# Block products of w_out and w_ffn_out in a decoder layer: eight multiplications of half-size blocks become seven

## The chip, the cores and the metric

One core of a Trainium2 chip runs the whole layer in one launch. The metric is the device time of one execution in microseconds (us); the kernel before took 893.11 us (median of three runs, 893.06 to 895.8).

## The reference, cut to what matters

One layer of a decoder works on 512 tokens with 1024 channels, all in float32. Only two of its many matrix products change, `merged @ w_out` and the second product of the SwiGLU:

```python
x = x + merged @ w_out[i]                          # 512x1024 @ 1024x1024
hf = rms_norm(x, norm_ffn[i]) @ w_ffn_in[i]
x = x + (jax.nn.silu(hf[..., :FFN_HIDDEN]) * hf[..., FFN_HIDDEN:]) @ w_ffn_out[i]   # 512x2816 @ 2816x1024
pg = jax.nn.sigmoid(rms_norm(x, norm_ple[i]) @ w_ple_gate[i])
x = x + pg * (p[i] @ w_ple_proj[i])
```

Ahead of them stand the input projection with its three branches (an SSM, a short convolution, sliding-window attention) and their gates; behind them the embedding gate (`w_ple_gate`) and a final norm.

## The kernel before, in words

Every float32 operand is split into two float32r parts, a high part `hi` (a copy by ACT, L206 for weights and L244 for activations) and the remainder `lo` (a subtraction by DVE, L207 and L245). A product is the sum of three matmuls, high by high, low by high and high by low (L248 to L250 where the result is channels by tokens, L1214 to L1216 where it is tokens by channels). So each 128x128 by 128x512 piece costs three matmuls.

Weights come as a stream of slabs of 1 MB (`add_slab`, L121). SP issues their loads (`emit_load`, L179, the DMA on L184) into two `raw` buffers. A slab is cut into two halves of 128x1024; `emit_split` (L187) writes the copy and, four steps later, the subtraction, into one of the pairs of `hi` and `lo` buffers: four pairs (`hla`) at first, seven from w_out on (`hlb`). `group` takes the next halves, `retire` and `ahead` write the split of a later half as soon as a pair of buffers is done with. So up to three halves (six later) are ready ahead of TensorE.

The order of work is written out by hand: each engine takes its instructions in program order, and a semaphore wait holds up everything behind it on that engine. `pump` counts three-matmul steps, and `later(d, fn)` puts an instruction of another engine d steps further on. A buffer that is used again makes its new writer wait until all readers of the old content are done.

The stages around the change are these. `branch` (L1145) makes `merged`, [1024 channels, 512 tokens], two 128-channel blocks at a time, each from 24 matmuls behind a gate product of 48, and splits them into `mh` and `ml`. `td_gemm` (L1230) multiplies them by w_out: four token tiles of 128 by two column halves of 512. Column half 0 runs with the weights outside (`td_outer_k`, four PSUM banks at once), column half 1 token tile by token tile; `accum` (L1209, the DVE addition on L1211) adds each finished bank into `xr`, the residual, which is loaded anew at L1205. After each tile of column half 1 `Norm.pre` (L1253) queues the norm of that tile: Square on ACT (L1261), mean on DVE (L1264), power on POOL (L1265), scaling on DVE (L1272) and eight transposes on PE (L325), at the steps 1, 3, 4, 9 and 10 of `NORM_AT`. The normed activations go into `h` and `l` (`hpool`, one buffer each, which hold the normed input of the whole first phase before).

The SwiGLU runs in three chunks of 8, 8 and 6 hidden 128-blocks (`CHUNKS`): a chunk makes its activations `gh`, `gl` from w_ffn_in (L1288 on) and multiplies them at once by its rows of w_ffn_out with `td_gemm`. The last chunk's column half 1 carries the norm for the embedding gate. That last stage needs `ppt` (2 MB) and a gain, both loaded in chunk 1.

Of the kernel before, what the change touches and what calls it, by code (L numbers as in the profile page):

```python
# [17 lines left out]
T = 512  # L18
D = 1024
# [56 lines left out]
def hybrid_trunk_kernel(  # L76
# [41 lines left out]
    halves = []  # L118
    slabs = []

    def add_slab(ap, k, n, axis):  # L121
        s = len(slabs)
        slabs.append(dict(ap=ap, k=k, n=n, raw=None))
        cnt = 2 if k * n == 2048 else 1
        for i in range(cnt):
            halves.append(dict(s=s, i=i, cnt=cnt, axis=axis, hl=None))
# [31 lines left out]
    for n in range(2):  # L158
        for kk in range(2):
            add_slab(kn(w_out[0][kk * 512:kk * 512 + 512, n * 512:n * 512 + 512]), 4, 512, "k")  # L160
    CHUNKS = [(0, 8), (8, 8), (16, 6)]
    for h0, hn in CHUNKS:
        for j in range(h0, h0 + hn, 2):
            for ab in range(2):
                c0 = ab * FFN + j * 128
                add_slab(kn(w_ffn_in[0][:, c0:c0 + 256]), 8, 256, "n")
        for n in range(2):
            for k0 in range(0, hn, 4):
                kq = min(4, hn - k0)
                r0 = (h0 + k0) * 128  # L170
                add_slab(kn(w_ffn_out[0][r0:r0 + kq * 128, n * 512:n * 512 + 512]), kq, 512, "k")
# [5 lines left out]
    state = dict(pump=0, delay=False, split=0, load=0, next=0, top=3, slot=0, pools=[hla] * 4)  # L177

    def emit_load():  # L179
        s = slabs[state["load"]]  # L180
        state["load"] += 1
        t = rawp.tile([128, 2048], F32, tag="raw", name="raw")
        v = t[:, 0:s["k"] * s["n"]].rearrange("p (k n) -> p k n", k=s["k"])
        sp.dma_start(out=v, in_=s["ap"])  # L184
        s["raw"] = v

    def emit_split():  # L187
        h = halves[state["split"]]
        state["split"] += 1
        while state["load"] <= h["s"]:  # L190
            emit_load()
        s = slabs[h["s"]]
        k, n, i = s["k"], s["n"], h["i"]
        if h["cnt"] == 1:
            src = s["raw"]
        elif h["axis"] == "n":
            n //= 2
            src = s["raw"][:, :, i * n:(i + 1) * n]
        else:
            k //= 2  # L200
            src = s["raw"][:, i * k:(i + 1) * k, :]
        pl = state["pools"][state["slot"] % len(state["pools"])]
        state["slot"] += 1
        hi = pl.tile([128, 1024], F32R, tag="hi", name="hi").rearrange("p (k n) -> p k n", k=k)
        lo = pl.tile([128, 1024], F32R, tag="lo", name="lo").rearrange("p (k n) -> p k n", k=k)
        act.copy(out=hi, in_=src)  # L206
        todo = [lambda: dve.tensor_tensor(lo, src, hi.bitcast(F32), ALU.subtract)]  # L207
        h["hl"], h["low"] = (hi, lo), lambda: todo and todo.pop()()
        later(LAG, h["low"])
# [177 lines left out]
    def prep_gen(tp):  # L387
        # per-channel vectors: ssm_d (4 tiles) and the conv taps (3 x 4 tiles)
# [59 lines left out]
    def prep_fine(tp, lt, ldt, T1, T2, tabs):  # L448
# [73 lines left out]
        # coefficients  # L522
# [85 lines left out]
    # the tensor engine's clock rises only under load  # L608
# [347 lines left out]
    # chunks of 4 tokens; channels of a group pair and the time in the chunk share the partitions  # L956
    def ssm_gen(ct):
# [69 lines left out]
        # the two row halves of the array write to banks of their own  # L1027
# [117 lines left out]
    def branch(d0, sgs, yh, yl, mode, mh=None, ml=None):  # L1145
        hl = take()
        for i in range(2):
# [8 lines left out]
            if mode == 2:  # L1156
                split_ap(merged[:, d], mh[:, d], ml[:, d])
# [42 lines left out]
    xp = open_pool(ctx, "xres")  # L1200
    hlb = open_pool(ctx, "hlb", 3)
    state["pools"] = [hla] * 4 + [hlb] * 3
    state["slot"] = 4
# [14 lines left out]
    def td_outer_k(ah, al, kn_, n):  # L1218
        pss = [ps_z() for _ in range(4)]
        for h in range(kn_ // 2):  # L1220
            hi, lo = take()
            for t in range(4):
                for k in range(2):
                    kk = 2 * h + k
                    td_mm(pss[t], ah, al, kk, slice(t * 128, (t + 1) * 128), hi, lo, k, kk == kn_ - 1)
                    pump()
        for t in range(4):
            accum(t, n, pss[t])

    def td_gemm(ah, al, kn_, pre_fn=None):  # L1230
        td_outer_k(ah, al, kn_, 0)
        if pre_fn is None:
            td_outer_k(ah, al, kn_, 1)
            return
        nh = kn_ // 2
        h0 = group(nh)
        for t in range(4):
# [184 lines left out]
```

## Time and profile before

| | us |
|---|---|
| median of 3 runs | 893.11 |
| span of the profiled execution, first to last instruction | 892.6 |
| TensorE busy in that span | 874.4 |
| VectorE, ScalarE, GpSimd busy | 491.1, 341.0, 95.9 |

The page gives the span of the profiled execution and no other time of it; the median lies 0.5 us above that span. PE is TensorE's matmuls, PEld its weight loads, DVE VectorE, ACT ScalarE, POOL GpSimd, SP the engine that issues the loads. Matmuls overlap in the pipeline, so the duration of one (0.39 us) is longer than the distance between the starts of two. A row of a timeline gives the start, the duration, the engine and the line; in square brackets stands how long the engine had been idle and who ended that.

### The profile page before, as it was taken

Reading aid. Unit: us, or ns where it says so; the run is one execution under the profiler, and the core shown is the slowest. Engines: PE = TensorE matmul, PEld = TensorE weight load, DVE = VectorE, ACT = ScalarE, POOL = GpSimd, SP = SyncE. Lnnn points to the kernel's source line nnn. Section 1 sums busy time; section 2 is a strip of 40 time slices with the busy share of each in tenths; the row PEclk is TensorE's granted clock in tenths of the full one; section 3 lists DMA queues with packets and bytes.
Section 4 is the critical chain, followed back from the end, with each engine's and each line's share of the span. In section 5 each row is a group of like instructions: output and inputs, shape, how many; then the busy total and the mean of one; then the engine's idle time right before and its main releaser. Section 6 shows DMA issues by size and latency. Waiting matters only on the chain.

```text
span 892.6 us, 10527 instructions
## 1 busy us (share of the span) xinstructions
PE 874.4 (98%) x4143; PEld 715.2 (80%) x4143; DVE 491.1 (55%) x737; ACT 341.0 (38%) x546; POOL 95.9 (11%) x86
## 2 busy tenths in 40 slices
PE   8999999999999979999999999999999999999997
PEld 6988787877777758888889888888888888888886
DVE  3789698948588585554545433333333333334654
ACT  5665556445443343433334322212222212222533
POOL 1030061713123030000000000000000000000000
PEclk9999999999999989999999999999999999999998
DMA  8756511253634523223813322222225332233002
GB/s 300 216 189 218 195 59 30 66 173 113 178 95 156 156 94 107 95 79 134 284 46 107 130 94 95 95 95 94 95 95 211 99 100 87 72 120 110 29 1 94
DMA packets 84849, 107.25 MB, mean 120 GB/s; under 512 B 6120, under 2 KB 66176, under 8 KB 84288
## 3 DMA queue, kind: packets, MB, share of 16 engines
q1 hardware_dynamic: 84800, 106.59, 36.5%
q8 instruction: 32, 0.52, 0.2%
q14 instruction: 17, 0.14, 0.1%
HBM read 94.83 MB, written 11.55 MB: 119 GB/s over the span
## 4 chain that ended last, share of the span: by engine, by line
PE 77%; DVE 10%; issue 4%; ACT 3%; DMA 3%; SPq 1%; POOL 1%; POOLq 0%; DVEq 0%; ACTq 0%
PE z L248 17%; PE z L249 16%; PE z L250 16%; PE z L1216 8%; PE z L1215 8%; PE z L1214 8%; DVE lo L207 1%; DVE s_t L839 1%; DMA xt<-in_x_dram 1%; PE t L325 1%; DVE s_t L812 1%; DMA raw<-in_w_in_dram 1%; POOL gsw L1063 1%; ACT s_t L826 1%; PE t L1084 1%
## 5 line engine op out<-in xcount | busy, mean ns | idle before, releaser
L248 PE MATMUL z<-h,hi 128*128 128x512 f32 (+1 forms) x776 | 298.6, 385 | 0.0
L207 DVE TENSOR_TENSOR lo<-raw,hi 128x1024 fp32r<-128x1024 f32 x142 | 177.6, 1253 | 216.2 <-ACT hi L206 216.1
L249 PE MATMUL z<-l,hi 128*128 128x512 f32 (+1 forms) x776 | 292.2, 377 | 0.0
L250 PE MATMUL z<-h,lo 128*128 128x512 f32 (+1 forms) x776 | 292.1, 376 | 0.0
L206 ACT CAST hi<-raw 128x1024 fp32r<-128x1024 f32 x142 | 148.2, 1047 | 133.1 <-PE z L1216 87.2
L248 PEld LDWEIGHTS z<-h,hi 128*128 128x128 f32 x776 | 146.8, 189 | 29.9 <-issue 3.7
L250 PEld LDWEIGHTS z<-h,lo 128*128 128x128 f32 x776 | 146.7, 189 | 27.6
L249 PEld LDWEIGHTS z<-l,hi 128*128 128x128 f32 x776 | 147.0, 189 | 24.7
L1214 PE MATMUL z<-hi,gh 128*128 128x512 f32 x176 | 69.5, 395 | 0.0
L1216 PE MATMUL z<-hi,gl 128*128 128x512 f32 x176 | 69.1, 393 | 0.0
L1215 PE MATMUL z<-lo,gh 128*128 128x512 f32 x176 | 69.1, 392 | 0.0
L1265 POOL TENSOR_TENSOR rs<-ms,nhalf 128x1 f32<-128x1 f32 x8 | 4.4, 550 | 487.2 <-DVE ms L1264 487.2
L244 ACT CAST gh<-sil 128x512 fp32r<-128x512 f32 x22 | 13.6, 620 | 86.0 <-DVE sil L1319 86.0
L248 PE MATMUL z<-yh,hi 128*128 128x512 f32 x112 | 45.1, 403 | 0.0
L249 PE MATMUL z<-yl,hi 128*128 128x512 f32 x112 | 44.2, 395 | 0.1
L250 PE MATMUL z<-yh,lo 128*128 128x512 f32 x112 | 44.2, 395 | 0.0
L1310 ACT ACTIVATE sil<-z 128x512 f32<-128x512 f32 x22 | 13.2, 598 | 75.4 <-PE z L250 75.4
L1319 DVE TENSOR_TENSOR sil<-z,sil 128x512 f32<-128x512 f32 x22 | 15.2, 691 | 46.8 <-PE z L250 46.8
L1216 PEld LDWEIGHTS z<-hi,gl 128*128 128x128 f32 x176 | 33.1, 188 | 7.5
L1215 PEld LDWEIGHTS z<-lo,gh 128*128 128x128 f32 x176 | 33.1, 188 | 7.4
L1214 PEld LDWEIGHTS z<-hi,gh 128*128 128x128 f32 x176 | 33.1, 188 | 7.3
L1211 DVE TENSOR_TENSOR xr<-z,xr 128x512 f32<-128x512 f32 x32 | 21.5, 687 | 15.6 <-PE z L1216 15.5
(258 smaller groups left out, 1058.5 us busy)
## 6 DMA issues: line engine op xcount, KB each, us to landing
raw<-in_w_in_dram SPq DMA_DIRECT2D x23, 1024.0 KB, 5.5
raw<-in_w_ffn_in_dram SPq DMA_DIRECT2D x22, 1024.0 KB, 5.2
raw<-in_w_ffn_out_dram SPq DMA_DIRECT2D x10, 1024.0 KB, 5.0
raw<-in_w_branch_dram SPq DMA_DIRECT2D x12, 512.0 KB, 3.4
cs<-tb SPq DMA_DIRECT2D x4, 1024.0 KB, 5.2
raw<-in_w_out_dram SPq DMA_DIRECT2D x4, 1024.0 KB, 5.8
raw<-in_w_ple_gate_dram SPq DMA_DIRECT2D x4, 1024.0 KB, 5.1
xt<-in_x_dram SPq DMA_DIRECT2D x4, 512.0 KB, 9.4
```

Source lines behind the costliest of these rows:

```text
L206: act.copy(out=hi, in_=src)
L207: todo = [lambda: dve.tensor_tensor(lo, src, hi.bitcast(F32), ALU.subtract)]
L244: act.copy(out=hi, in_=src)
L248: pe.matmul(ps, wh, ah, start=first, stop=False)
L249: pe.matmul(ps, wh, al, start=False, stop=False)
L250: pe.matmul(ps, wl, ah, start=False, stop=last)
L1211: dve.tensor_tensor(dst, ps, dst, ALU.add)
L1214: pe.matmul(ps, ah[:, kk, ts], hi[:, k, ns], start=(kk == 0), stop=False)
L1215: pe.matmul(ps, ah[:, kk, ts], lo[:, k, ns], start=False, stop=False)
L1216: pe.matmul(ps, al[:, kk, ts], hi[:, k, ns], start=False, stop=last)
L1310: act.activation(out=s, in_=ps, func=AF.Silu)
L1319: dve.tensor_tensor(sil[i], ps, sil[i], ALU.mult)
```

## The change: what it does, and the diff

The four products (w_out, and the three chunks of w_ffn_out) are written as 2 by 2 blocks: two halves of 256 tokens, two halves of the inner dimension (alternating 128-blocks, `kt` of them each: 4, 4, 4 and 3) and two column halves of 512. Seven block products with sums of blocks take the place of eight. The sums of activation blocks are made by DVE in `forms`, which splits seven blocks (`fh`, `fl`) for each pair of 128-blocks in place of two. The sums of weight blocks are made by DMAs: `x` is B12, and B11 is added to it by a second DMA with `accum_op` ADD; when `x` has been split, B22 is added to it (`x+`), and when that has been split, B21. `y` is B12 plus B22. These DMAs are issued by POOL. A block product serves two token tiles, adds into PSUM banks that several products share, and after each product DVE adds the bank into `xr` or subtracts it. `x` and `y` of w_out lie in the buffers `h` and `l` of `hpool`; those of the chunks lie in a pool of their own and are issued four slabs early (`early=4`; 0 for w_out). The seven pairs of split buffers stay four until the embedding gate; `ppt` comes in four loads after chunk 2.

```diff
+    def add_block_product(w, r0, kt, early=4):
+        def blk(h, n):
+            v = w[r0:r0 + 2 * kt * 128, n * 512:n * 512 + 512].rearrange("(i h p) n -> h p i n", h=2, p=128)
+            return v[h]
+        at = len(loads) - early
+        kinds = (("raw", blk(0, 0)), ("raw", blk(1, 0)), ("x", (blk(0, 1), blk(0, 0))), ("raw", blk(1, 1)),
+                 ("x+", blk(1, 1)), ("y", (blk(0, 1), blk(1, 1))), ("x+", blk(1, 0)))
+        for kind, ap in kinds:
+            add_slab(ap, kt, 512, "k", kind, at if kind in ("x", "y") else None)
+
+    add_block_product(w_out[0], 0, 4, 0)
...
+        add_block_product(w_ffn_out[0], h0 * 128, hn // 2)
...
     def emit_load():
...
+            pl, tag = state["xy"][s["kind"]]
+            t = pl.tile([128, 2048], F32, tag=tag, name=s["kind"])
...
+            pool.dma_start(out=v, in_=s["ap"][0])
+            pool.dma_start(out=v, in_=s["ap"][1], accum_op=ALU.add)
...
+    def more_x(s):
+        for q in slabs[s + 1:s + 8]:
+            if q["kind"] == "x+" and q["raw"] is None:
+                pool.dma_start(out=state["x"], in_=q["ap"], accum_op=ALU.add)
...
+        def low():
+            dve.tensor_tensor(lo, src, hi.bitcast(F32), ALU.subtract)
+            if s["kind"] in ("x", "x+") and h["i"] == h["cnt"] - 1:
+                more_x(h["s"])
...
-            if mode == 2:
-                split_ap(merged[:, d], mh[:, d], ml[:, d])
+        if mode == 2:
+            forms(merged[:, d0:d0 + 2], d0 // 2)
...
+    def forms(g, i):
+        sums = fmp.tile([128, 4, 256], F32, tag="sums", name="sums")
+        g11, g12, g21, g22 = (g[:, h, o:o + 256] for o in (0, 256) for h in range(2))
+        split_ap(g[:, :, 0:256], fh[:, 0:2, i], fl[:, 0:2, i])
+        dve.tensor_tensor(sums[:, 0], g21, g22, ALU.subtract)
+        dve.tensor_tensor(sums[:, 1], sums[:, 0], g11, ALU.subtract)
+        dve.tensor_tensor(sums[:, 2], g11, g21, ALU.subtract)
+        dve.tensor_tensor(sums[:, 3], g12, sums[:, 1], ALU.add)
+        split_ap(sums, fh[:, 3:7, i], fl[:, 3:7, i])
+        split_ap(g22, fh[:, 2, i], fl[:, 2, i])
...
-    hlb = open_pool(ctx, "hlb", 3)
-    state["pools"] = [hla] * 4 + [hlb] * 3
...
+    PRODUCTS = ((A11, 0, True, 1, 0, 0), (A12, 2, True, 1, 0, 0), (FD, 1, True, 1, 1, 1), (S4, 1, False, 1, 0, 1),
+                (S2, 0, False, -1, 0, 1), (S3, 0, False, -1, 1, 1), (A22, 0, False, 1, 1, 0))
+
+    def block_product(kt, norm=None):
+        banks = {}
+        for i, (f, bk, first, sign, th, n) in enumerate(PRODUCTS):
+            if first:
+                banks[bk] = [(ps_t if bk == 2 else ps_z)() for _ in range(2)]
+            for q in range(2):
+                h0 = group(1)
+                if q == 0:
+                    ahead()
+                hi, lo = halves[h0]["hl"]
+                k0, kc = halves[h0]["part"][0:2]
+                for t in range(2):
+                    ps, ts = banks[bk][t], slice(t * 128, (t + 1) * 128)
+                    for k in range(kc):
...
+                        pe.matmul(ps, fh[:, f, kk, ts], hi[:, k], start=st, stop=False, skip_group_check=True)
+                        pe.matmul(ps, fl[:, f, kk, ts], hi[:, k], start=False, stop=False, skip_group_check=True)
+                        pe.matmul(ps, fh[:, f, kk, ts], lo[:, k], start=False, stop=last, skip_group_check=True)
+                        pump()
+                    if last:
+                        dst = xr[:, 2 * th + t, n * 512:(n + 1) * 512]
+                        dve.tensor_tensor(dst, ps if sign > 0 else dst, dst if sign > 0 else ps,
+                                          ALU.add if sign > 0 else ALU.subtract)
+                        if norm is not None and i in (4, 6):
+                            norm.pre(2 * th + t)
+                retire(h0)
...
-    td_gemm(mh, ml, 8, nf.pre)
+    block_product(4, nf)
...
-        if ci == 2:
-            td_gemm(gh, gl, hn, npl.pre)
-        else:
-            td_gemm(gh, gl, hn)
+            forms(g, j // 2)
+        block_product(hn // 2, npl if ci == 2 else None)
...
+    hlb = open_pool(ctx, "hlb", 3)
+    state["pools"] = [hla] * 4 + [hlb] * 3
...
+    for t in range(4):
+        sp.dma_start(out=ppt[:, t], in_=pp_d[t * 128:(t + 1) * 128, :])
```

## Rows read from the trace of the kernel before

**Rows 1.** The page: span, and busy time of the engines

```profile
span 892.6 us, 10527 instructions
...
PE 874.4 (98%) x4143; PEld 715.2 (80%) x4143; DVE 491.1 (55%) x737; ACT 341.0 (38%) x546; POOL 95.9 (11%) x86
```

**Rows 2.** Stretches: PE, PEld, DVE, ACT, POOL busy (count), PEclk, DMA share, GB/s

```profile
423.90:468.20 44.30, 44.30 (x201) 36.10 (x201) 22.00 (x28) 15.12 (x21) 1.66 (x3) 1.00 0.48 166
641.00:682.00 41.00, 41.00 (x180) 33.58 (x179) 14.11 (x15) 10.88 (x14) 0.00 (x0) 1.00 0.25 83
```

**Rows 3.** Groups by line and form: count, busy us, mean ns, then idle before

```profile
L207 DVE TENSOR_TENSOR lo<-raw,hi 128x1024 fp32r<-128x1024 f32 x142 | 177.6, 1253 | 216.2 <-ACT hi L206 216.1
L206 ACT CAST hi<-raw 128x1024 fp32r<-128x1024 f32 x142 | 148.2, 1047 | 133.1 <-PE z L1216 87.2 <-DMA raw<-in_w_in_dram 19.8 <-PE z L249 16.3
...
L1214 PE MATMUL z<-hi,gh 128*128 128x512 f32 x176 | 69.5, 395 | 0.0
...
L1214 PE MATMUL z<-hi,mh 128*128 128x512 f32 x64 | 25.5, 398 | 0.0
...
L1211 DVE TENSOR_TENSOR xr<-z,xr 128x512 f32<-128x512 f32 x32 | 21.5, 687 | 15.6 <-PE z L1216 15.5
...
L245 DVE TENSOR_TENSOR gl<-sil,gh 128x512 fp32r<-128x512 f32 x22 | 15.2, 693 | 15.3 <-ACT gh L244 15.3
```

**Rows 4.** Timeline of PE: last gate matmul, first of w_out, end of w_out's column half 0

```profile
418.13 0.39 PE L250 MATMUL z<-h,lo 128*128 128x512 f32 x1
...
423.95 0.39 PE L1214 MATMUL z<-hi,mh 128*128 128x512 f32 x1
...
446.00 0.39 PE L1216 MATMUL z<-hi,ml 128*128 128x512 f32 x1
```

**Rows 5.** Timeline of w_out's column half 1: a finished bank, its addition, the norm

```profile
451.54 0.39 PE L1216 MATMUL z<-hi,ml 128*128 128x512 f32 x1
...
451.97 0.69 DVE L1211 TENSOR_TENSOR xr<-z,xr 128x512 f32<-128x512 f32 x1 [3.23 <-PE z L1216]
...
452.70 1.06 ACT L1261 ACTIVATE xn<-xr 128x1024 f32<-128x1024 f32 x1 [5.21 <-DVE xr L1211]
...
454.11 0.55 POOL L1265 TENSOR_TENSOR rs<-ms,nhalf 128x1 f32<-128x1 f32 x1 [102.72 <-DVE ms L1264]
...
454.70 1.29 DVE L1272 SCALAR_TENSOR_TENSOR xn<-xr,rs,g 128x1024 f32<-128x1024 f32 x1 [0.66 <-POOL rs L1265]
```

**Rows 6.** DMA issues: count, KB of each, median us from issue to landing

```profile
raw<-in_w_ffn_out_dram SPq DMA_DIRECT2D x10, 1024.0 KB, 5.0
...
raw<-in_w_out_dram SPq DMA_DIRECT2D x4, 1024.0 KB, 5.8
...
xt<-in_x_dram SPq DMA_DIRECT2D x4, 512.0 KB, 9.4
...
xr<-in_x_dram SPq DMA_DIRECT2D x1, 2048.0 KB, 7.9
```

**Rows 7.** DMA queues, in GB/s, in 40 slices of 416 to 424 us

```profile
GB/s 0 0 0 0 0 184 82 41 51 338 338 410 399 420 399 420 399 420 399 420 389 215 0 0 0 0 0 0 0 0 0 0 0 0 0 0 0 0 0 0
```

**Rows 8.** Timeline of SP's queue at the start of w_out

```profile
424.14 0.37 SPq L1205 DMA_DIRECT2D xr<-in_x_dram  x1
424.56 0.50 SPq L331 DMA_DIRECT2D g<-in_norm_ffn_dram  x1
```

**Rows 9.** Timeline of PE where it stood longest behind the start

```profile
324.61 0.80 PE L1082 MATMUL t<-uu,Dg 128*128 128x128 f32 x2 [4.49 <-ACT Dg L1075]
```

**Rows 10.** Stretches around rows 9, columns as in rows 2

```profile
320.00:322.00 2.00, 0.12 (x1) 0.00 (x0) 1.98 (x3) 1.09 (x3) 0.87 (x1) 1.00 0.00 0
324.00:326.00 2.00, 1.39 (x4) 0.79 (x4) 0.84 (x2) 1.58 (x3) 1.53 (x1) 0.50 0.18 35
328.00:330.00 2.00, 2.00 (x9) 1.35 (x8) 1.90 (x3) 0.63 (x1) 0.03 (x1) 0.50 0.50 173
330.00:332.00 2.00, 2.00 (x11) 1.44 (x11) 1.97 (x4) 0.00 (x0) 0.00 (x0) 0.90 0.23 34
```

More of the change, by code (lines that the diff above doesn't have):

```diff
@@ L119, in hybrid_trunk_kernel, with add_slab @@
     slabs = []
-    def add_slab(ap, k, n, axis):
+    loads = []
+    def add_slab(ap, k, n, axis, kind="raw", load=None):
         s = len(slabs)
[L123 to L126, printed above, removed]
+        slabs.append(dict(ap=ap, k=k, n=n, raw=None, kind=kind))
+        if kind != "x+":
+            loads.insert(len(loads) if load is None else load, s)
+        if k * n <= 1024:
+            parts = [(0, k, 0, n)]
+        elif axis == "n":
+            parts = [(0, k, i * (n // 2), n // 2) for i in range(2)]
+        else:
+            k1 = (k + 1) // 2
+            parts = [(0, k1, 0, n), (k1, k - k1, 0, n)]
+        for i, q in enumerate(parts):
+            halves.append(dict(s=s, i=i, cnt=len(parts), part=q, hl=None))
     def kn(ap):
@@ L157, in hybrid_trunk_kernel @@
         add_branch(0, pair)
-    for n in range(2):
-        for kk in range(2):
-            add_slab(kn(w_out[0][kk * 512:kk * 512 + 512, n * 512:n * 512 + 512]), 4, 512, "k")
+    A11, A12, A22, FD, S2, S3, S4 = range(7)
+    def add_block_product(w, r0, kt, early=4):
[8 more added lines that the diff above has]
+    add_block_product(w_out[0], 0, 4, 0)
     CHUNKS = [(0, 8), (8, 8), (16, 6)]
@@ L176, in hybrid_trunk_kernel @@
     due = {}
[L177 removed]
+    state = dict(pump=0, delay=False, split=0, load=0, next=0, top=3, slot=0, pools=[hla] * 4, xy=None, x=None)
+    state["xy"] = dict(x=(hpool, "h"), y=(hpool, "l"))
     def emit_load():
[L180 removed]
+        s = slabs[loads[state["load"]]]
         state["load"] += 1
[L182 to L185 removed]
+        if s["kind"] == "raw":
+            t = rawp.tile([128, 2048], F32, tag="raw", name="raw")
+        else:
+            pl, tag = state["xy"][s["kind"]]
+            t = pl.tile([128, 2048], F32, tag=tag, name=s["kind"])
+        v = t[:, 0:s["k"] * s["n"]].rearrange("p (k n) -> p k n", k=s["k"])
+        if s["kind"] == "raw":
+            sp.dma_start(out=v, in_=s["ap"])
+        else:
+            pool.dma_start(out=v, in_=s["ap"][0])
+            pool.dma_start(out=v, in_=s["ap"][1], accum_op=ALU.add)
+            if s["kind"] == "x":
+                state["x"] = v
+        s["raw"] = v
+    def more_x(s):
+        for q in slabs[s + 1:s + 8]:
+            if q["kind"] == "x+" and q["raw"] is None:
+                pool.dma_start(out=state["x"], in_=q["ap"], accum_op=ALU.add)
+                q["raw"] = state["x"]
+                return
     def emit_split():
@@ L1230, in td_gemm @@
[L1230 to L1237, printed above, removed]
-            ahead()
-            ps = ps_z()
-            for kk in range(kn_):
-                hi, lo = halves[h0 + kk // 2]["hl"]
-                td_mm(ps, ah, al, kk, slice(t * 128, (t + 1) * 128), hi, lo, kk % 2, kk == kn_ - 1)
-                pump()
-                if t == 3 and kk % 2:
-                    retire(h0 + kk // 2, kk == 1)
-            accum(t, 1, ps)
-            pre_fn(t)
+    PRODUCTS = ((A11, 0, True, 1, 0, 0), (A12, 2, True, 1, 0, 0), (FD, 1, True, 1, 1, 1), (S4, 1, False, 1, 0, 1),
+                (S2, 0, False, -1, 0, 1), (S3, 0, False, -1, 1, 1), (A22, 0, False, 1, 1, 0))
@@ new lines, in block_product @@
+    def block_product(kt, norm=None):
[12 more added lines that the diff above has]
+                    for k in range(kc):
+                        kk = k0 + k
+                        st = first and kk == 0
+                        last = kk == kt - 1
+                        pe.matmul(ps, fh[:, f, kk, ts], hi[:, k], start=st, stop=False, skip_group_check=True)
[9 more added lines that the diff above has]
+                retire(h0)
```

88 lines of the change are left out of this document (32 added, 56 removed).

## The prediction, made before the changed kernel ran

> **What bounds the kernel now.** I read the page first: PE is busy for 874.4 of 892.6 us and no other engine for more than 55% [rows 1]. Then the stretches, since a share over the whole span hides stages: in w_out and in the SwiGLU, PE is busy all the time at the full clock, DVE half and a third of it, the DMAs half and a quarter [rows 2]. Third, the groups by line: the 720 matmuls of w_out (64 on each of L1214 to L1216) and w_ffn_out (176 on each) show no idle time of PE in front of them [rows 3]. So both products are bound by the number of matmuls, as long as weights are split in time. The price of one matmul is not its 0.39 us but the distance of starts: 96 of them lie between 423.95 and 446.00 us, 22.05 / 95 = 0.232 us [rows 4]. I use 0.23.
>
> The sum is made against the profiled span of 892.6 us, 0.5 below the median of 893.1; differences go onto the median.
>
> **Removed.** Seven of eight block products stay: 720 becomes 630 matmuls, 90 x 0.23 = 20.7 us less, all on PE's path; 24 x 0.23 = 5.5 of it in w_out. The count stands in the code, so the change cannot fail to do this.
>
> **Added beside PE.** A half of weights now feeds 12 matmuls (2.76 us), not 24. Per half, ACT does one copy (1.05) and DVE one subtraction (1.25) and on average one bank addition (0.69) [rows 3]: 1.94 of 2.76 us on DVE. That fits, but where DVE was idle half of the time it is now used to 70%, in the last chunk, where a block is split two and one 128-blocks at a time, to 80%. `forms` adds per pair four DVE sums of half-size tiles (about 0.4 each, estimated from the 0.69 of L245) and some 1.2 us of splitting: 3 us per pair, against a pair's 22 us of SwiGLU matmuls, DVE being free two thirds of them [rows 2]. I cost it at nothing; if that cover were gone it would be 15 x 3 = 45 us. Four buffer pairs instead of seven cost nothing in w_ffn_in: refilling takes 1.05 + 1.25 and three halves, 16 us, stand ahead. `ppt` and its gain now arrive on SP's queue after chunk 2, but a late one holds DVE's additions only; five PSUM banks of 5.5 us each cover it. The weight loads of a product of size 4 grow from 4 to 9 MB, 18.75 MB in all over the 420 us from here on: some 45 GB/s on top of about 100, far from full [rows 2].
>
> **Turns of a bank, +3.1.** New is that three products (S4 behind FD, S3 behind S2, A22 behind S3) write into a bank that DVE has just read for its addition. After the last matmul of a token tile has started, DVE starts 0.43 us later and takes 0.69 [rows 5]; then stands a subtraction of 1.25, then the second tile's addition of 0.69: done after 3.06 us. PE wants that bank 13 matmuls on, after 2.99. Three products of size 4 have three such turns; I take 0.25 us each for the missing 0.07 and the semaphore. With size 3 PE is back after 4 x 0.23 = 0.92, the first addition is done after 1.12: 0.3 each. Together 9 x 0.25 + 3 x 0.3 = 3.1 (bounds 0 and 12 x 0.69 = 8.3).
>
> **The wait for x in w_out, S.** This decides. `x` and `y` of w_out lie in `h` and `l`, which the last gate product reads until 418.5 [rows 4]. Only then can POOL issue y's load, and behind it, on one queue and each add waiting for its load: y's add, x's load, x's add. PE gets to x after two products: 423.95 + 48 x 0.23 = 435.0; as copy and subtraction stand ahead of its third matmul, x must land by 435.4 - 2.3 = 433.1. No row shows a load from POOL or an adding one. For a plain 1 MB load the bounds are 5.0 and 9.4 [rows 6]; I take 5.8, that of w_out. Of it 1.05 MB / 420 GB/s = 2.5 is transfer [rows 7] and 3.3 the rest. For an add of 1 MB, A, the least is 5.0 and the most two loads end to end, 11.6. It touches HBM and the tile, so it is nearest to the 2 MB of xr with 7.9; between 5.8 and 7.9 I take 6.8. Beside it SP loads xr and a gain from 424.1 on [rows 8], 2.6 MB or 6.2 us of the same engines; I put half ahead, 3.1. So x lands at 418.5 + 5.8 (y) + (A - 3.3) (y's add) + 2.5 (x) + 3.1 + 3.3 + A = 429.9 + 2A, and S = 2A - 3.2: 10.4 us at A = 6.8.
>
> Behind x's two additions of B22 and B21 (the second and third add) PE has room at first: in a chunk, x's last half is split some 8 us in, product 4 starts at 22, so an add up to 11 us is hidden. In w_out the norm is tighter: it waits behind ACT's copy of the third add. With x landed at X, splits take 3.55 twice, so the third add lands at X + 7.1 + 2A; a copy (1.05) and the norm's 3.3 (452.70 to 455.99 [rows 5]) make X + 11.5 + 2A, and PE reaches the transposes at about X + 26. Above A = 7.2 each us costs two. In chunk 2 an add moves 3/4, and the same working gives a limit of 6.5 for it, A = 7.6. POOL's power (0.55) stands behind these DMAs on its queue but is called later than they are issued.
>
> **The clock, +2.8.** Where PE stood 4.5 us [rows 9], PEclk fell from 1.00 to 0.50, which is 1.2 for 2.4 GHz, and was back only at about 330, so 5.6 us ran at half [rows 10]: 2.8 lost. A wait of 10 us will do the same once.
>
> **Sum.** -20.7 + 3.1 + 10.4 + 2.8 = -4.4: **888.7 us**.
>
> The Trainium skill, in Collectives: The Full Stack, "The bandwidth ceiling: the fold count and why AG ≠ RS ≠ AR", says that a DMA which adds reads two sources on one ring and so moves data at half the rate. By it the add's transfer would be 5.0 us instead of 3.5, and the sum that of the second rival. No row here shows an add.
>
> **Rivals.**
>
> 1. *The wait in w_out hardly binds.* POOL's DMAs get the engines ahead of SP, and an add costs as a load does. Then S = 2 x 5.0 - 3.2 - 3.1 = 3.7, a wait too short for the clock: -20.7 + 3.1 + 3.7 = -13.9, 879. For it: SP's 2.6 MB are not needed before x. Against: six transfers in 15 us behind one another. Chance 0.12.
>
> 2. *An add takes its transfer twice,* A = 3.3 + 5.0 = 8.3: S = 13.4; the norm of w_out loses 2 x 1.1 = 2.2, chunk 2 (its add 7.05) 1.1; -20.7 + 3.1 + 13.4 + 2.8 + 3.3 = +1.9: 895. Here stands the skill's rule, named above. Chance 0.24: the nearest row, 7.9, lies close to it.
>
> 3. *Slower: POOL's adding queue becomes the bound.* Where it bites is w_out's three adds in a row, its price four us for each us of A, and from A = 7.9 on it outweighs the matmuls saved (at 7.9: -14.8 + 12.6 + 1.4 + 0.5 = 0). At A = 10: S = 16.8, norm 5.6, chunk 2 (8.3) 3.6; -20.7 + 3.1 + 16.8 + 2.8 + 9.2 = +11.2: 904. For it: POOL has to make the transfers itself, and no row prices that. Against: 40% more than two sizes' worth of data explains. Chance 0.24.
>
> The forecast has 0.40.
>
> **How the numbers follow.** A measurement of this kernel can tell about 0.3%, 2.7 us, from no change. The forecast, with A between 5.8 and 7.4, gives 886.7 to 890.5 and counts as faster but for its upper edge (0.02); of rival 2, 0.15 lies within 0.3% and 0.09 above. Faster 0.12 + 0.38 = 0.50, the same 0.02 + 0.15 = 0.17, slower 0.09 + 0.24 = 0.33. The range goes from 879 (rival 1) to 905 (rival 3 at A = 10); outside are adds beyond 10 us and waits that I have not seen. The forecast's own range is 884 to 891.
>
> **What would show it.** Right: 630 matmuls on three new lines, 0.23 apart in the three chunks; in w_out one idle time of PE of about 10 us some 11 us in, ended by ACT's copy, that one by a DMA into x, and PEclk at half behind it; turns of about 0.3 us, released by DVE. Wrong: the DMAs' time to landing (5.8 for the load, 6.8 for the add) tells which rival holds; idle time of PE in the chunks that ACT's copy ends would mean that the adds are late there too; DVE above 80% with PE waiting for subtractions would mean that the cover I counted on is gone; and a chunk whose matmuls start more than 0.25 us apart would void the first term.

## The result, and the profile after

The changed kernel takes **929.14 us** (median of four runs, 927.96 to 933.76) beside 893.7 for the kernel before in the same runs: a ratio of 1.0399, 95% interval 1.0379 to 1.0418. It is 35 us slower, outside the range of the prediction. The profiled span is 926.2 us, 33.6 above the one before.

The page, the PE waits and the stretches behind PE's stops, all of the changed kernel. First the page: span, busy times, the queue of POOL's loads and adds (packets, MB, share of 16 engines' span), and three rows of DMA issues (count, KB, median us to landing), to be set beside [rows 1] and [rows 6].

```profile
span 926.2 us, 10635 instructions
...
PE 866.4 (94%) x4053; PEld 704.0 (76%) x4053; DVE 563.1 (61%) x862; ACT 375.6 (41%) x587; POOL 122.7 (13%) x110
...
q0 software_dynamic: 9984, 23.59, 12.3%
...
x<-in_w_ffn_out_dram POOLq DMA_DIRECT2D x8, 1024.0 KB, 9.7
...
raw<-in_w_ffn_out_dram SPq DMA_DIRECT2D x6, 1024.0 KB, 5.1
...
x<-in_w_out_dram POOLq DMA_DIRECT2D x4, 1024.0 KB, 8.7
```

PE has 90 matmuls fewer and is busy for 94% instead of 98% of a longer span. POOL's transfers into `x`, loads and adds together, land after 8.7 and 9.7 us, SP's loads of blocks of the same size after 5.1. The view of PE's waits (total us, times, longest) says what it stood for:

```profile
PE z L1293 <- DVE xr L1299: 20.3, 6, 7.2
PE z L1293 <- ACT hi L244: 17.6, 1, 17.6
...
PE t L369 <- DVE l L289: 2.9, 2, 2.6
```

L1293 is the first matmul of a block product, L1299 the addition of a bank into `xr`, L244 the copy of weights by ACT, L369 a transpose of the norm. Only the wait of 17.6 us, for `x` in w_out, is the one that the prediction had; of the six on DVE's additions four are far longer than the 0.3 us that it gave a turn of a bank. The third view is of stretches behind the stops (PE, PEld, DVE, ACT, POOL busy, granted clock, DMA share, GB/s):

```profile
452.00:456.00 4.00, 3.96 (x11) 2.58 (x11) 4.00 (x5) 2.30 (x3) 1.26 (x1) 0.56 0.00 0
...
466.00:470.00 4.00, 3.31 (x8) 2.63 (x9) 1.77 (x3) 0.77 (x1) 1.27 (x1) 0.50 0.00 0
470.00:474.00 4.00, 4.00 (x14) 3.14 (x13) 1.78 (x3) 0.66 (x2) 0.00 (x0) 0.68 1.01 169
606.00:610.00 4.00, 4.00 (x12) 3.08 (x11) 0.43 (x2) 1.04 (x1) 1.27 (x1) 0.61 0.34 36
736.00:740.00 4.00, 3.32 (x8) 2.64 (x9) 1.76 (x3) 0.79 (x1) 1.27 (x1) 0.50 0.00 0
740.00:744.00 4.00, 4.00 (x15) 3.16 (x14) 1.80 (x3) 0.81 (x2) 0.00 (x0) 0.72 1.08 174
...
860.00:866.00 6.00, 5.91 (x22) 4.86 (x23) 3.50 (x4) 0.95 (x2) 0.00 (x0) 0.58 0.33 90
```

Behind each of the five longest stops the clock is at the lower of its two levels (0.50, which is 1.2 of 2.4 GHz) for 3 to 6 us. The time lost, estimated as PE's busy time times what is missing of the clock: 1.7, 1.7, 1.3, 1.6, 1.7, 1.1 and 2.5, together 11.6 us.

Read from PE's timeline, from the first matmul of a stage to the end of its last one, w_ffn_in being what lies between (the idle column adds up PE's waits inside it; the last column is run e12, below):

| stage, us | before | after | of it idle | e12 |
|---|---|---|---|---|
| w_out | 46.4 | 71.2 | 24.3 | 46.7 |
| chunk 0 of w_ffn_out | 44.3 | 44.7 | 3.5 | 40.6 |
| chunk 1 | 44.4 | 45.4 | 3.3 | 40.6 |
| chunk 2 | 35.3 | 43.0 | 8.1 | 35.5 |
| product of the last stage | 47.4 | 51.1 | 3.2 | 47.0 |
| w_ffn_in, three stretches | 244.5 | 242.0 | 0 | 242.2 |

So -20.7 for the matmuls, +42.3 idle and +11.6 of clock make +33.2, against 33.6 in the spans. The match hides two amounts that cancel: the five stages of the table are some 4 us longer than these terms make them, and w_ffn_in and the stretch ahead of w_out (it begins at 422.32, not 423.95) are 2.5 and 1.6 us shorter.

The 2.5 us in w_ffn_in, which isn't changed, can be read from PE's starts. A half of weights feeds 24 matmuls there; these are the first of three halves running in the kernel before:

```profile
632.49 0.39 PE L248 MATMUL z<-h,hi 128*128 128x512 f32 x1
...
637.93 0.40 PE L248 MATMUL z<-h,hi 128*128 128x512 f32 x1
...
643.51 0.39 PE L248 MATMUL z<-h,hi 128*128 128x512 f32 x1
```

The first half takes 5.44 us, the second 5.58. Of every seven halves running four take 5.43 to 5.48 and three 5.56 to 5.60; in the changed kernel and in e12 every half takes 5.44 to 5.45. Four and three are the pairs of split buffers in `hla` and `hlb`, and the change opens `hlb` only for the last stage. So this gain seems to belong to which buffers hold the weights and not to the block products; that it is the place of the buffers is inferred from the counts, and no run tried the kernel before with four pairs.

**Where the waits come from.** In chunk 0 one timeline shows a chain through four engines. POOL issues the second add to `x`; ACT's copy of that sum waits for it; DVE's subtraction waits for ACT; the addition of a finished bank stands behind that subtraction on DVE; PE wants that bank.

```profile
593.55 1.27 POOL L222 DMA_DIRECT2D x<-in_w_ffn_out_dram  x1 [74.59 <-DVE lo L247]
...
602.37 1.99 ACT L244 CAST hi<-x 128x1024 fp32r<-128x1024 f32 x2 [6.66 <-DMA x<-in_w_ffn_out_dram]
...
599.09 0.69 DVE L1299 TENSOR_TENSOR xr<-z,xr 128x512 f32<-128x512 f32 x1 [2.04 <-PE z L1295]
603.45 1.23 DVE L247 TENSOR_TENSOR lo<-x,hi 128x1024 fp32r<-128x1024 f32 x1 [3.66 <-ACT hi L244]
604.59 0.68 DVE L1299 TENSOR_TENSOR xr<-z,xr 128x512 f32<-128x512 f32 x1
...
605.33 0.51 PE L1293 MATMUL z<-hi,fh 128*128 128x512 f32 x1 [3.48 <-DVE xr L1299]
```

The add took 602.37 - 593.55 = 8.8 us. PE has just begun S4 (its weights are the plain B22) and wants the sum only for the product behind it, S2, which without a stop begins eight halves of 2.76 us into the chunk, at 583.49 + 22.1 = 605.6; what is late is the addition at 604.59, which has nothing to do with the sum. The Trainium skill, in PSUM — Partial Sum Buffer, "Engine vs sequencer instructions", says that the queues of ScalarE, VectorE and GpSimd are strictly first in, first out; by that rule, the trace agrees: DVE stood 3.66 us with that addition behind it.

In w_out the queues of POOL and SP show why `x` is late, and ACT when it is there:

```profile
417.00 0.96 POOL L212 DMA_DIRECT2D y<-in_w_out_dram  x1 [67.23 <-PE z L294]
423.32 1.29 POOL L213 DMA_DIRECT2D y<-in_w_out_dram  x1 [5.37 <-DMA y<-in_w_out_dram]
424.10 1.30 POOL L212 DMA_DIRECT2D x<-in_w_out_dram  x1
441.89 1.28 POOL L213 DMA_DIRECT2D x<-in_w_out_dram  x1 [16.49 <-DMA x<-in_w_out_dram]
...
422.52 0.37 SPq L1259 DMA_DIRECT2D xr<-in_x_dram  x1
422.94 0.50 SPq L375 DMA_DIRECT2D g<-in_norm_ffn_dram  x1
...
450.41 1.99 ACT L244 CAST hi<-x 128x1024 fp32r<-128x1024 f32 x2 [22.54 <-DMA x<-in_w_out_dram]
```

`y` loads in 6.3 us; `x`, beside y's add, the 2 MB of `xr` and the gain, in 17.8; x's add, nearly alone, takes 450.41 - 441.89 = 8.5. In that time the DMA engines are full, and do less when they add:

```profile
427.00:443.00 16.00, 6.92 (x30) 5.26 (x28) 3.04 (x4) 0.88 (x1) 1.11 (x1) 0.86 1.01 295
443.50:450.00 6.50, 0.00 (x0) 0.00 (x0) 0.00 (x0) 0.00 (x0) 0.00 (x0) 0.50 0.97 161
```

### The profile page after: what moved, and what is told of

The parts are those of the page before. It is cut to its first block, busy times and chain, and to the rows that moved or that the text cites. A ratio compares the mean times of both kernels' runs of the same rounds, so it can differ in the third digit from the quotient of the medians.

```text
span 926.2 us, 10635 instructions
## 1 busy us (share of the span) xinstructions
PE 866.4 (94%) x4053; PEld 704.0 (76%) x4053; DVE 563.1 (61%) x862; ACT 375.6 (41%) x587; POOL 122.7 (13%) x110
## 3 DMA queue, kind: packets, MB, share of 16 engines
q0 software_dynamic: 9984, 23.59, 12.3%
## 4 chain that ended last, share of the span: by engine, by line
PE 69%; DVE 12%; DMA 10%; ACT 4%; issue 4%; POOL 1%; SPq 0%; POOLq 0%; DVEq 0%; ACTq 0%
PE z L292 18%; PE z L294 17%; PE z L293 17%; DMA x<-in_w_out_dram 4%; DMA x<-in_w_ffn_out_dram 3%; DVE lo L247 3%; PE z L1293 3%; PE z L1294 2%; PE z L1295 2%; PE z L1270 1%; PE z L1269 1%; PE z L1268 1%; PE z L686 1%; ACT hi L244 1%; PE t L369 1%
## 5 line engine op out<-in xcount | busy, mean ns | idle before, releaser
L247 DVE TENSOR_TENSOR lo<-raw,hi 128x1024 fp32r<-128x1024 f32 (+1 forms) x136 | 168.3, 1240 | 118.5 <-ACT hi L244 118.3
L244 ACT CAST hi<-raw 128x1024 fp32r<-128x1024 f32 (+1 forms) x136 | 140.7, 1038 | 97.7 <-PE z L293 30.8
L1293 PE MATMUL z<-hi,fh 128*128 128x512 f32 x180 | 76.9, 427 | 38.3 <-DVE xr L1299 20.3
L1295 PE MATMUL z<-lo,fh 128*128 128x512 f32 x180 | 75.1, 417 | 0.6 <-DVE lo L247 0.5
L1294 PE MATMUL z<-hi,fl 128*128 128x512 f32 x180 | 75.3, 419 | 0.0
L1293 PEld LDWEIGHTS z<-hi,fh 128*128 128x128 f32 x180 | 36.3, 202 | 50.5 <-ACT hi L244 18.3
L247 DVE TENSOR_TENSOR lo<-x,hi 128x1024 fp32r<-128x1024 f32 (+1 forms) x24 | 27.5, 1152 | 39.6 <-ACT hi L244 39.6
L244 ACT CAST hi<-x 128x1024 fp32r<-128x1024 f32 (+1 forms) x24 | 23.0, 990 | 68.5 <-DMA x<-in_w_out_dram 34.0
L293 PE MATMUL z<-yl,hi 128*128 128x512 f32 x112 | 44.2, 395 | 0.1
L294 PE MATMUL z<-yh,lo 128*128 128x512 f32 x112 | 44.2, 395 | 0.0
L1295 PEld LDWEIGHTS z<-lo,fh 128*128 128x128 f32 x180 | 36.2, 201 | 10.5 <-DVE lo L247 1.7
L1294 PEld LDWEIGHTS z<-hi,fl 128*128 128x128 f32 x180 | 36.4, 202 | 8.7 <-DVE fl L289 0.8
L1299 DVE TENSOR_TENSOR xr<-z,xr 128x512 f32<-128x512 f32 x32 | 21.8, 687 | 25.6 <-PE z L1295 22.4
```

What stands on the lines that cost most here:

```text
L293: pe.matmul(ps, wh, al, start=False, stop=False)
L294: pe.matmul(ps, wl, ah, start=False, stop=last)
L1293: pe.matmul(ps, fh[:, f, kk, ts], hi[:, k], start=st, stop=False, skip_group_check=True)
L1294: pe.matmul(ps, fl[:, f, kk, ts], hi[:, k], start=False, stop=False, skip_group_check=True)
L1295: pe.matmul(ps, fh[:, f, kk, ts], lo[:, k], start=False, stop=last, skip_group_check=True)
L1299: dve.tensor_tensor(dst, ps if sign > 0 else dst, dst if sign > 0 else ps, ALU.add if sign > 0 else ALU.subtract)
```

## The experiments

Theory A: the adds take about 8 to 10 us; the split of a sum stands in order on ACT and DVE in front of bank additions, and so stops PE earlier than the sum itself is wanted; in w_out the DMA engines are full; the longer stops cost clock. The rivals are named with each run. In the order of the change x serves FD, with B22 added S2, with B21 added A22; y serves S3. Each ratio is to the kernel before in the same set of runs, where it took 893.7 to 895.6 us.

### Which part loses: e4

w_out as before, the chunks as block products.

```diff
-    add_block_product(w_out[0], 0, 4, 0)
+    for n in range(2):
+        for kk in range(2):
+            add_slab(kn(w_out[0][kk * 512:kk * 512 + 512, n * 512:n * 512 + 512]), 4, 512, "k")
...
-    block_product(4, nf)
+    td_gemm(mh, ml, 8, nf.pre)
```

> The changed kernel with w_out as it was before the change (raw weights, 192 matmuls, four tiles of hi and lo instead of seven), the chunks as block products. By the stages of the two traces w_out's stage lost about 24 us and the chunks with what follows some 11. Theory A: w_out's stage is 46 to 52 us again instead of 71, and the time is 904 to 910: the chunks alone still lose to the kernel before, 893.7. Rival F (the chunks alone gain, and only w_out loses): under 892. Rival G (the loss moves on to the first chunk, whose x and y then collide with something else): over 918.

903.34 us (ratio 1.0083, 1.0068 to 1.0098), just under Theory A's 904. w_out's stage is 46.7 us, without a wait, and the chunks lose as they did: some 26 of the 35 us belong to w_out. F and G fall.

### What an add costs: e3

```diff
-            pool.dma_start(out=v, in_=s["ap"][1], accum_op=ALU.add)
+            pool.dma_start(out=v, in_=s["ap"][1])
...
-                pool.dma_start(out=state["x"], in_=q["ap"], accum_op=ALU.add)
+                pool.dma_start(out=state["x"], in_=q["ap"])
```

> The changed kernel with every adding load made a plain load to the same place (so the weight sums are left out: x, y and the later x are the last block loaded); the same number of transfers, in the same order, with the same waits. Theory A in its first half (adding costs more than loading): each load that follows takes about 6 instead of 8.5 to 10 us; then PE's waits on DVE xr in the chunks go (limit 6.5 us), and the time is 905 to 915. Rival E (adding is as quick as loading, and what is late is the chain of dependent loads on POOL's queue): the loads take 8 to 10 us as before and the time stays over 924.

902.87 us (1.0081, 1.0062 to 1.0101), 2 under the range of Theory A: the same transfers in the same order without the adding are worth 26 us. Its queue and issue rows and PE's wait on the additions, beside those of the changed kernel above:

```profile
q0 software_dynamic: 6144, 23.59, 7.3%
...
x<-in_w_ffn_out_dram POOLq DMA_DIRECT2D x8, 1024.0 KB, 6.5
...
x<-in_w_out_dram POOLq DMA_DIRECT2D x4, 1024.0 KB, 5.7
...
PE z L1293 <- DVE xr L1299: 7.0, 5, 4.3
```

Of the 24 transfers on this queue 16 add in the changed kernel. Here a transfer takes 7.3% of 901.5 us / 24 = 2.74 us of all engines; there 12.3% of 926.2 = 113.9, less 8 x 2.74 for the loads, leaves 5.75 for each add: **2.1 times a load**. The packets say the same: 6144 / 24 = 256 a load, (9984 - 8 x 256) / 16 = 496 an add. The Trainium skill's rule from Collectives: The Full Stack, "The bandwidth ceiling: the fold count and why AG ≠ RS ≠ AR", that an add reads two sources and halves the rate, is stated there for the ring of a ReduceScatter; these rows agree with it for a load into one core. E falls. Of the 20.3 us that PE waited on additions 7.0 are left, 4.3 of them in chunk 2 and 2.0 in w_out, where a plain load is late too. In the first two chunks the idle time is 0.3 us and nothing, their products take 39.9 and 39.7 us; chunk 2 still has 4.7 us of idle time, and w_out a wait of 10.5 for `x`.

### Late sums, or a queue: e5, e2, e6

e5 is e4 and one condition in `ahead`: the first half of a later sum goes to ACT and DVE one half later.

```diff
+        for q in range(state["split"], min(last, len(halves) - 1) + 1):
+            if slabs[halves[q]["s"]]["kind"] == "x+" and q > state["next"] + 2:
+                last = q - 1
+                break
```

> Run e4 (w_out as before, chunks as block products in the change's own order) with one line more: the first half of a block that comes out of a later add (the second and third x sum) is handed to ScalarE and VectorE one half later, that is, behind the additions of the bank that PE takes up again, not in front of them. Nothing else moves: the same transfers, the same products, the same sums. Theory A (queues in program order: the split that waits for the add stands in front of the additions into xr): PE's waits on DVE xr in the chunks, 3.1, 2.9 and 7.8 us in e4, fall to under 0.5 each in the first two and to 4 or less in the third, because the sum itself is there in time for its own product; time 892 to 896 beside e4's 903.3. Rival H (the sum is too late for its own product as well): the same waits come back two products on, as PE's wait on ACT hi or DVE lo, and the time stays over 900.

896.71 us (1.0017, 1.0005 to 1.0029), 6.6 less than e4 and 0.7 above Theory A's range. DVE in chunk 0 now has both bank additions in front of the split that waits:

```profile
577.38 0.69 DVE L1306 TENSOR_TENSOR xr<-z,xr 128x512 f32<-128x512 f32 x1 [2.04 <-PE z L1302]
578.78 0.69 DVE L1306 TENSOR_TENSOR xr<-z,xr 128x512 f32<-128x512 f32 x1 [0.71 <-PE z L1302]
581.18 2.36 DVE L249 TENSOR_TENSOR lo<-x,hi 128x1024 fp32r<-128x1024 f32 x2 [1.71 <-ACT hi L246]
```

Chunks 0 and 1 take 40.4 and 40.8 us instead of 44.2 and 43.8, with 0.6 and 0.9 idle, though the add is as slow (571.83 to 580.10, 8.3 us). So there the sum was in time and the queue was the loss; H falls for them. Chunk 2 keeps 7.5 us of idle time, against the 4 or less that Theory A gave it; read from the trace, and not tested alone: with three 128-blocks a product is shorter, and the norm of the upper rows stands on DVE between the late copies and the additions as well.

e2 leaves the queues and gives the adds time, by another order of the products in the chunks, FD first and S2 ahead of S4:

```diff
+    TURN = (2, 0, 1, 4, 3, 5, 6)
...
+        for i, (f, bk, first, sign, th, n) in enumerate(PRODUCTS if turn is None else [PRODUCTS[j] for j in turn]):
```

> The changed kernel with the seven products of the three chunks in another order (FD, A11, A12, S2, S4, S3, A22): the same sums, but two products instead of one lie between the uses of the first and the second x sum, and of the second and the third, and one bank instead of three is used by two products running. w_out is unchanged. Theory A (the add-loads take 8 to 10 us and the split of the summed weights stands on VectorE and ScalarE in front of the additions into xr): PE's waits on DVE xr in the chunks (3.5, 3.3 and 7.2 us) go, and the falls of the clock behind them; the chunks' products go from 44.5, 45.2 and 42.8 us to about 40, 40 and 33. Time about 910 to 914. Rival B (VectorE's work is too much for the chunks): waits of the same sum, time over 924. Rival D (the adding loads run at half the rate whenever the next chunk's loads run beside them, and are late in any order): half of it stays, 920.

916.1 us (1.0231, 1.0216 to 1.0246), 13 below the change and 2 above the range of Theory A. PE's longest waits in the chunks are these:

```profile
PE z L1297 <- DVE xr L1303: 3.2, 1, 3.2
PE z L1298 <- DVE fl L293: 2.3, 3, 0.8
```

The chunks take 40.6, 40.6 and 36.7 us; B and D fall, but the 3.2 us before chunk 2's last product, which A wanted gone, stay. New is a wait of 0.8 us in each chunk for the form FD, which `forms` splits among its last and this order uses first.

> Run e4 with the turned order of e2 in the chunks. If the parts add up: e4's 903.3 less the 13 us that e2 took off, 890. Left by theory A: 4 us of idle time before the last product of the third chunk and the norm behind it, so that the first two chunks are 3.7 us shorter than in the kernel before and the third with the last stage some 6 longer. Rival B (VectorE): over 898.

e4's and e2's edits together give 892.87 us (0.9984, 0.997 to 0.9999), 3 above the sum of the parts, hardly to be told from the kernel before; B falls. Chunks 0 and 1 are 40.6 each; chunk 2 with the last stage, 38.3 + 51.1, is 6.6 longer than before. That stretch is left.

### w_out: e1, e14, e8, e11

> The changed kernel with one thing turned round: each product's x is put in the list of loads ahead of its y (in the change y is ahead, though x is wanted three products sooner). Theory A (the sums are late, and w_out's x is late because its load runs beside y's add and the load of the rows of x): x's load starts at about 417 with nothing of POOL beside it, x lands near 433 instead of 450, and the 17.6 us of PE's wait on ACT hi in w_out go down to 3 or less; the chunks stay as they are. Time about 909 to 913. Rival B (the matrix engine is held by VectorE's load, not by the loads): the wait stays in some other form, over 922. Rival C (x's load is slow whatever runs beside it, 17 us): x lands near 443, time about 918 to 922.

```diff
-            add_slab(ap, kt, 512, "k", kind, at if kind in ("x", "y") else None)
+            add_slab(ap, kt, 512, "k", kind, at + (kind == "y") if kind in ("x", "y") else None)
```

922.24 us (1.0303, 1.0285 to 1.032), a miss. `x` did come at 437.6 and the wait for it fell to 5.4 us, but what was taken from one wait went to the next:

```profile
441.24 1.28 POOL L213 DMA_DIRECT2D y<-in_w_out_dram  x1 [16.32 <-DMA y<-in_w_out_dram]
442.00 1.81 POOL L222 DMA_DIRECT2D x<-in_w_out_dram  x1
...
456.45 1.99 ACT L244 CAST hi<-x 128x1024 fp32r<-128x1024 f32 x2 [15.02 <-DMA x<-in_w_out_dram]
...
459.41 0.79 PE L1293 MATMUL z<-hi,fh 128*128 128x512 f32 x1 [10.84 <-DVE xr L1299]
```

The time is the one of rival B, but not for its reason: from 446 to 456 us DVE was busy for 0.50 of 10 us, while the DMA engines were full (columns as in the stretches above).

```profile
446.00:456.00 10.00, 2.57 (x12) 1.72 (x10) 0.50 (x1) 0.00 (x0) 0.00 (x0) 0.74 1.11 229
```

C falls, since x was quick. Now y's load took 17.6 us in the crowded stretch, and y's add ran beside the second add to `x`, which needed 14.5 us; again the bank additions stood behind its split.

> The changed kernel without the add to y in w_out (y stays its first block, so this one weight sum is left out); everything else is the change. Theory A (the sixteen DMA engines are full from 427 to 443, and an add takes them twice as long as a load): the add's 2 MB of engine time are gone from the stretch in which x loads, x's load takes about 11 to 12 us instead of 17.5, x lands near 444 instead of 450, PE's wait for it falls from 17.6 to 11 or 12 us; time 921 to 924. Rival M (the rows of x and the gain alone hold x's load): x's load stays over 15 us, time 927 or more. Rival N (y's add alone held it): x's load takes 6 to 7 us, the wait falls to 6 us, under 918.

```diff
+            if s["kind"] == "x" or state["xy"]["y"][1] == "y":
                 pool.dma_start(out=v, in_=s["ap"][1], accum_op=ALU.add)
```

919.03 us (1.0268, 1.0246 to 1.0291), between A and N; M falls. The wait for `x` is 7.0 us, but not in the way that I had expected: without y's add, which waited on POOL's queue for y's load, x's load is issued 1 us behind y's load instead of 7 and takes 8.1 us, and x's add is now the one beside the rows of x.

```profile
419.23 0.96 POOL L212 DMA_DIRECT2D y<-in_w_out_dram  x1 [67.23 <-PE z L295]
420.18 0.79 POOL L212 DMA_DIRECT2D x<-in_w_out_dram  x1
428.28 1.32 POOL L214 DMA_DIRECT2D x<-in_w_out_dram  x1 [7.31 <-DMA x<-in_w_out_dram]
...
442.02 1.99 ACT L245 CAST hi<-x 128x1024 fp32r<-128x1024 f32 x2 [11.91 <-DMA x<-in_w_out_dram]
```

That add took 13.7 us instead of 8.5. So both seem to crowd `x`: the rows of x by some 5 us, y's add by its data and by its place on the queue, which this run doesn't separate.

e8 takes the loads out of the crowd: `x` and `y` of all four products in buffers of the last branch that are free after the GLU gate, x issued ahead of y as in e1, all four products in the turned order.

```diff
+    wx, wy = y_tiles()
+    state["fixed"] = dict(x=wx.rearrange("p a b -> p (a b)").bitcast(F32), y=wy.rearrange("p a b -> p (a b)").bitcast(F32))
...
-    add_block_product(w_out[0], 0, 4, 0)
+    add_block_product(w_out[0], 0, 4, 3)
```

> All four as block products in the turned order, and x and y in two buffers of the last branch that are free after the GLU gate, so that w_out's two sums can be loaded during the last gates instead of after them. Theory A: no wait for x in w_out, its stage 42 to 45 us instead of 71; time 886 to 891. Rival J (in w_out the second x sum still comes late, because the rows of x, 2 MB, run beside it): a wait of 5 us or more at the fourth product, 893 to 898.

891.61 us (0.9969, 0.9956 to 0.9981). x's load starts at 374.5, w_out takes 46.2 us instead of 71.2, and no wait for `x` or its second sum is left; J falls. But the 46.2 are no less than the 46.4 before and above the 42 to 45 of Theory A, whose time is missed by 0.6: 3.9 us are idle, for the forms and for weights behind an addition that waited for `xr`. e11 shows the latter most plainly. It's e10 (below: e8 with chunk 2 in the old form) with the order turned once more:

```diff
-    PRODUCTS = ((FD, 1, True, 1, 1, 1), (A11, 0, True, 1, 0, 0), (A12, 2, True, 1, 0, 0), (S2, 0, False, -1, 0, 1),
+    PRODUCTS = ((A11, 0, True, 1, 0, 0), (FD, 1, True, 1, 1, 1), (A12, 2, True, 1, 0, 0), (S2, 0, False, -1, 0, 1),
```

> Run e10 with A11 ahead of FD: the FD form is the last one that VectorE makes, and in e6 and e8 PE waits 0.76 us for it at the start of each chunk, in w_out 1.4 us. Theory A: 1.5 us less in the two chunks and 1.5 to 3 in w_out: 881 to 884. If the second x sum then comes too late again (one product less between): a wait of 2 us or more at the fourth product, and no gain.

```profile
438.39 0.69 DVE L1305 TENSOR_TENSOR xr<-z,xr 128x512 f32<-128x512 f32 x1 [8.62 <-DMA xr<-in_x_dram]
439.00 1.22 DVE L252 TENSOR_TENSOR lo<-raw,hi 128x1024 fp32r<-128x1024 f32 x1
```

With A11 first, its bank is added sooner; that addition waits 8.6 us for the rows of x, weights stand behind it, PE stops 5.5 us, and w_out takes 53.4 us. The two chunks went down to 39.6 as expected, but the run came to 888.15 (0.9934), 3 above e10.

### The last stage: e7, e12, e9, e10, e13

e7 is e6 with chunk 2 in the old form:

```diff
+        if hn == 8:
+            block_product(hn // 2, None, TURN)
+        else:
+            td_gemm(gh, gl, hn, npl.pre)
```

> Run e6 with the third chunk as before the change too (raw weights, 144 matmuls): block products in the first two chunks alone. Theory A: the third chunk and the last stage take 83 us as in the kernel before instead of 89, the first two chunks about 40.6 instead of 44.3 each: 883 to 886, faster than the kernel before by 1%. Rival I (the norm of the last stage is late because of the changed pools, not because of the order of the rows): no better than e6.

897.28 us (1.0032, 1.0021 to 1.0044): 4 above e6, a miss. Chunk 2 is 35.5 us as expected, but the last stage takes 59.0, so rival I holds. SP's queue, ACT and DVE:

```profile
829.23 0.34 SPq L388 DMA_DIRECT2D g<-in_norm_final_dram  x1
829.62 1.96 SPq L1439 DMA_DIRECT2D ppt<-pp  x4
831.69 2.25 SPq L223 DMA_DIRECT2D raw<-in_w_ple_gate_dram  x2
...
841.55 1.04 ACT L257 CAST hi<-raw 128x1024 fp32r<-128x1024 f32 x1 [11.24 <-DMA raw<-in_w_ple_gate_dram]
842.50 1.05 ACT L1361 ACTIVATE xn<-xr 128x1024 f32<-128x1024 f32 x1
...
845.99 1.09 PE L382 MATMUL t<-cst,xn 128*128 128x128 f32 x4 [9.67 <-DVE xn L1372]
```

The gain and `ppt` are issued only at 829.2, when chunk 2's matmuls have ended and its memory is free; the gate's weights stand behind them on SP. ACT, with seven pairs of buffers, has the split of those weights ahead of the square (L1361) of the last row tile. It's the same pattern as in the chunks, one stage on. e12 leaves those three extra pairs out:

```diff
-    hlb = open_pool(ctx, "hlb", 3)
-    state["pools"] = [hla] * 4 + [hlb] * 3
-    state["slot"] = 4
```

> Run e7 (two chunks as block products, w_out and chunk 2 as before) with four tiles of hi and lo in the last stage. In e7 ScalarE stood 11.2 us on a split that waited for the third slab of the gate's weights, and the square of the last row tile behind it; PE waited 9.7 us for that tile's norm and its clock fell. Theory A: that wait goes, the last stage takes 47 to 48 us instead of 59, time 885 to 887. Rival L (the gate's weights themselves are late, since the loads of pp and the gain wait for memory in front of them on SP's queue): the wait moves to the product, over 893.

**884.77 us** (0.9888, 0.9871 to 0.9905), faster than both kernels, beside the kernel before by 1.1%; the last stage takes 47.0 us. SP issues as late as in e7 (830.48), so L falls: ACT begins the square of the last row tile at 832.55, 0.96 us after its last work, and not behind a split that waits.

e9 is e8 with this edit, e10 is e9 with that of e7, e13 is e12 with that of e11.

> Run e8 with four tiles of hi and lo in the last stage as in the stages before it (the change takes up three more there, in memory that chunk 2 has just left, so that its splits of the gate's weights look three halves further ahead). Theory A (the norm's squares and the additions stand behind splits that wait): part of the 3.2 us of idle time in the last stage and of the 3.2 us before the last product of chunk 2 goes, 887 to 890 beside e8's 891.6. Rival K (these waits come from the order of the rows alone: both lower row tiles end with the last product): nothing moves, 891 to 892.

892.81 us (0.9973, 0.9954 to 0.9992), 0.1% from e8, which is no change: K holds. The waits before chunk 2's last product and in the last stage (3.2 each) stay with four pairs; they go only where chunk 2 is done in the old form, whose row tiles end one after the other:

> Run e9 with chunk 2 as before the change (raw weights, the row tiles ending one after the other): w_out and two chunks as block products. By e6 and the kernel before, chunk 2 and the last stage are 35.3 and 47.4 us in the old form, 39.3 and 51.1 in e8: 884 to 886. If the 9.7 us wait of e7 (the square of the last row tile behind a split that waited for the gate's weights) comes back although the splits look less far ahead, 892 or more.

885.17 us (0.9895, 0.9877 to 0.9914). That is as expected. Beside e12 it has w_out as a block product as well, and gains nothing by it: w_out takes 47.9 us here and 46.7 there.

> Run e12 with A11 ahead of FD, as in e11. In e11 the two chunks took 39.6 us without any wait, against 40.6 in e12. Theory A: 2 us less than e12, 882 to 883.5, and the chunks' products are then 4.7 us each under the kernel before, of the 5.5 us of 24 matmuls at 0.23 us. If the wait for the last form had cost only itself, 1.5 us: 883.3; if the second x sum comes too late with one product less between, over 885.

884.96 us (0.9887, 0.987 to 0.9904), the same as e12 and not the 2 us less of Theory A: the chunks are 0.4 and 0.7 us shorter, with waits of 0.5 and 0.3 for the second sum's remainder in place of 0.8 for the form.

## Why the prediction was wrong, point by point

- **Matmuls, -20.7: right.** 630 stand on three lines; where nothing stops them their starts are 0.23 apart.
- **Turns of a bank, +3.1: too high.** Where no split is late (chunks 0 and 1 of e3) PE waits at one turn of three, 0.3 and 0.1 us; in the turned order (e12) at none.
- **Forms and DVE at nothing: nearly right.** No wait in the changed kernel is for a form; where FD comes first, 0.8 us in a chunk of size 4 and 1.4 in chunk 2 and w_out. Four pairs of buffers in w_ffn_in were put at nothing too; with them it got 2.5 us shorter.
- **The price of an add, A = 6.8: low.** Alone it took 8.3 to 8.8 us: rival 2's price of 8.3, and its reason, twice the transfer. But with A = 8.5 the prediction's own working (S = 13.8, norm 2.6, chunk 2 1.4) gives +3.0, 896; the rest of the 35 us comes by the next steps, and that rival's 895 was wrong by them as well.
- **The step that failed: "so an add up to 11 us is hidden".** I asked when the sum is wanted by its own product and not what else stands behind its split on ACT and DVE, though three halves of look-ahead put it a product and a half early. Of the 20.3 us on `xr`, in w_out and the chunks, 13.3 go when nothing adds (e3). e5 shows the step for chunks 0 and 1, since the same add then costs PE 0.6 and 0.9 us; for w_out it's read from the traces. In chunk 2 it's a part of the 7.2 us: 3.2 stay when the sums are in time (e2, e9), and in the trace the norm of the upper rows then stands on DVE in front of the additions.
- **The wait for x in w_out, 10.4: mis-sized, 17.6.** y's load (6.3 for 5.8) and x's add (8.5 for 6.8) hold within 2 us; x's load was put at 12.4 with queueing and took 17.8. I had let half of SP's transfers, 3.1 us, stand ahead of it and y's add hold the engines for A - 3.3 = 3.5; with all 6.2 and e3's 5.75 the same working gives 5.75 + 6.2 + 2.5 + 3.3 = 17.8, an estimate, and the engines were full from 427 to 443.
- **The norm: left out.** For w_out and chunk 2 I had limits for A; I had none for the last stage, whose lower two row tiles both end with the last product. Cost: 3.2 us idle and the clock (e9, e10).
- **The clock, +2.8, once: 11.6.** The price of a stop was about right (1.6 to 2.9), their number was not. Rival 1 took 3.7 us for too short a wait; behind the stops of 3.3 and 3.5 the clock was at its lower level.

With measured terms, -20.7 + 42.3 + 11.6 = +33.2. The range ended at 905 because "waits that I have not seen" were left out of it, and such waits made more than half of the idle time.

## What to carry to other kernels

A transfer that is late need not stop its own reader first: it can stop, earlier, whatever was written behind that reader on an in-order queue. So for every new wait, list what is queued behind it within the look-ahead, and take the earliest due time of those as the limit. An algorithm that saves multiplications by dependent loads paid here only where the first loads have a stage ahead of them and two products lie between the later ones: in two chunks of four products, 7.5 of the 9.9 us gained in e12 (2.3 more came in w_ffn_in, with the four pairs of buffers). Sums for w_out were not worth having, even loaded ahead of the 16 us of crowded DMA engines (e8).

## What the runs showed of the hardware

An adding DMA takes the DMA engines 2.1 times as long as a load of the same size, in 1.9 times the packets (e3), and the issue of the later adds to `x` takes POOL 1.26 us, of plain loads in their place 0.75. Behind stops as short as 3.3 and 3.5 us TensorE's clock was at its lower level for 3 to 6 us (rows above); the stops of 3 to 7 us cost another 1.6 to 2.9 us each. In w_ffn_in 24 matmuls take 5.44 or 5.58 us, by the half of weights they use. Left open: why the halves differ, and what `xr` loaded earlier would bring to w_out, which wasn't tried.
